# The last plain c and x step of a decoder layer written as a pair of products, with four attention tiles kept in DRAM

## The chip, the cores and the metric

The kernel is one program on one core of a Trainium2 chip. The metric is the device time of one execution in microseconds; lower is better. The engines are named as the profile names them: PE (TensorE, matmuls), PEld (its weight loads), DVE (VectorE), ACT (ScalarE), POOL (GpSimd) and SP (SyncE, which here only issues DMA).

## The reference

One layer of a hybrid decoder runs over 512 prompt tokens and 8 x 8 decode tokens, 576 columns in all, with model width 1024 and everything in fp32. Cut to what matters:

```python
h = _rmsnorm(x, norm1_g) * (1.0 + sc1) + sh1
proj = h @ w_in        # columns: b_gate, c_gate, xa (1024 each), q 1024, k 256, v 256, ga, gb (1024 each)
u = c_gate * xa
uc, new_conv = _causal_conv(u, conv_buf, conv_w)          # width 3
ya = (b_gate * uc) @ w_conv_out
o, k_state, v_state = attend(q, k, v, attn_sinks)         # window 128, 16 heads in 4 groups, sinks, ALiBi
yb = o @ w_attn_out
mixed = sigmoid(ga) * ya + sigmoid(gb) * yb
x = x + g1 * (mixed @ w_mix_out)
h2 = _rmsnorm(x, norm2_g) * (1.0 + sc2) + sh2
a, val = split(h2 @ w_up)
ac, new_ffn = _causal_conv(a, ffn_buf, ffn_conv_w)
x = x + g2 * ((gelu(ac) * val) @ w_down)
```

The outputs are the two results, the new convolution states, and the last 128 key and value rows of the prompt and of each decode sequence.

## The kernel before

**Products.** Activations lie transposed: 1024 channels are 8 tiles (`k`) of 128 partitions by 576 token columns. A column tile `m` of a weight matrix is 128 outputs wide and is loaded as one tile `raw` of 128 x 1024. An fp32 product is made of three passes with operands that are split into a high part and a low part: high weights by high activations, high by low, low by high. Splitting is a rounding on ACT (`whi <- raw`) and a subtraction on DVE (`wlo <- raw, whi`). A plain product (`product`) runs 8 k by 3 passes by the 2 column groups 0:256 and 256:576, 48 matmuls.

**Pairs.** `pair_product` computes two plain products by seven products of half the depth on half the columns, in the manner of Strassen and Winograd: seven parts of 4 k by 3 passes on 288 columns, 84 matmuls, into the three PSUM banks X, Y and Z. Between the parts, ACT writes a bank's negative into another (`minus`), and evictions (`out_a0`, `out_a1`, `out_b0`, `out_b1`) add or subtract the copy `p5`. The activations' sums (`t`, `n1`, `n3`, `n4`) are made once. Each pair needs its own weight operands: two raw tiles and their sums, in the steps `sums1 ah al bh bl dh dl sums2 ch cl` of `pair_weights`. A letter in its argument `moved` chooses another engine for a low part: for "D", ACT writes the negated high part into `wl` and POOL issues a DMA that adds the fp32 tile `s` to it. A `Job` holds one pair: `load` issues its raw loads on SP, `prepare` gives the weight steps by the number of the part behind which they stand.

**The order of the work around the change.** The first projections are six plain steps, `for at, m in enumerate(PLAIN)`. Each is a product for c, a product for x, their elementwise product `u`, and the short convolution of `u`. Beside steps 1 to 3 the queries come as three pairs (`Q_PAIRS`). Then come 18 jobs, all pairs: 14 on `w_in` and 4 on `w_conv_out`. While a job runs, the next one is prepared and the one after that is loaded. Attention is a generator that is advanced by `tick`, which every k of a product and the first k of every part calls: `filler[1]` is the rate of attention steps by tick, .4 in the last plain step and .35 from the decode tokens on. It interleaves scores (`aux <- kh, q`), a softmax on DVE and ACT, the turn of the probabilities on TensorE by the identity (`aux <- ident, s`), their copies `pt` and the products with V (`aux <- pt, V`). `prompt_values` copies attention's results to the tiles `ot` (two for each of the four key heads), which stay on the chip until the attention output product reads them after the jobs.

A scheduler orders the instructions of an engine, except where the engine is in the list `pinned`: its instructions then stay in the order of the code. POOL's and SP's loads in this stretch are in program order too. In before PE, ACT and DVE join the list ahead of the last plain step's x product. There are 57 tiles of 128 x 576 or less to share (`A_BUFS`), 4 raw tiles, 5 tiles each for high and low weights, and PSUM banks in two groups, `mm` and `aux`.

In the profile most operations carry one line, L114, since a helper records them; after the change it is L115. The results' copies `ot` are L1196 (after: L1199), the products with V L1185 (L1187), the cache copies to the output on POOL L1476 (L1490).

Of the kernel before, what the change touches and what calls it, by code (L numbers as in the profile page):

```python
# [10 lines left out]
F32 = mybir.dt.float32  # L11
# [5 lines left out]
P = 128  # L17
D = 1024
NK = D // P
# [11 lines left out]
ROWS_AHEAD = 5  # L31
PLAIN = (0, 1, 2, 4, 5, 6)
Q_TICKS = 8
Q_PAIRS = (1,2,3,)
OPS_AT = 1, 2, 3, 4
CACHE_AT = 17,18
# [38 lines left out]
def step_kernel(ctx: ExitStack, tc: tile.TileContext, ins: dict, outs: list):  # L75
    nc = tc.nc
# [18 lines left out]
    def slot(s, dt=F32, shape=None):  # L95
        return ap_.tile(shape or [P, NT], dt, tag="a", name=nm(s))
# [7 lines left out]
    pinned = []  # L104
# [78 lines left out]
    def weights(src, nk):  # L183
        return split_w(load_w(src, nk))
# [305 lines left out]
    def pair_product(w, x, steps, out_a0, out_a1, out_b0, out_b1, apart=False):  # L490

        X, Y = (halves(mmps())[1][:, :HT] if apart or n else aux()[:, :HT] for n in range(2))
        Z = aux()[:, :HT]
        p5 = slot("p5")[:, :HT]

        def part(bank, wn, xn_, more=True):

            (hi, lo), xs = w[wn], x[xn_]  # L500
            for k in range(4):
                xh, xl = xs[k]
                passes = (hi(k), xh), (hi(k), xl), (lo(k), xh)
                for n, (wt, xx) in enumerate(passes):
                    matmul(
                        bank, wt, xx, start=not more and k + n == 0, stop=k + n == 5,
                        skip_group_check=more,
                    )
                if k == 0:
                    tick(2)  # L510

        def minus(out, src):
            act.activation(out, src, AF.Copy, scale=-1.0)

        parts = [
            (X, "a0", "x00", lambda: minus(Y, X)),
            (Z, "s1", "n1", lambda: act.copy(p5, Z)),
            (Y, "s2", "t2", lambda: minus(Z, Y)),
            (X, "a1", "x10", lambda: out_a0(X)),
            (Y, "s3", "n3", lambda: out_b1(Y, p5, ALU.subtract)),  # L520
            (Z, "s4", "x11", lambda: out_a1(Z, p5, ALU.add)),
            (Y, "b1", "n4", lambda: out_b0(Y)),
        ]
        if 0 in steps:
            steps[0]()
        for at, (bank, wn, xn_, after) in enumerate(parts):
            part(bank, wn, xn_, at > 1)
            after()
            if at + 1 in steps:
                steps[at + 1]()  # L530

    def kpm(w, m0, k0=0, nk=NK):
        return w[k0 * P : (k0 + nk) * P, m0 : m0 + P].rearrange("(k p) m -> p k m", p=P)
# [476 lines left out]

    pinned.append(pe)
    ot = []
    od = []

    def softmax_steps(s, n, sinks, nsinks, w):
# [161 lines left out]
    def prompt_values(parts):  # L1177
        O = aux()
        while len(ot) < 2 * parts[-1][0] + 2:
            ot.append(slot("ot"))  # L1180
        for u, (hd, i, pts) in enumerate(parts):
            nkt, c = len(pts), slice(256 * u, 256 * u + 256)
            for n in range(2 * nkt):
                kt, par = n // 2, n % 2
                done = nc.tensor.matmul(  # L1185
                    O[HALF[par], c],
                    vt(i - nkt + 1 + kt)[:, hd * 64 : hd * 64 + 64],  # L1187
                    pts[kt][:, par * 256 : par * 256 + 256],
                    start=(kt == 0), stop=(kt == nkt - 1),
                )  # L1190
                if u + n:
                    tc.keep_in_program_order(done)
        for u, (hd, i, pts) in enumerate(parts):
            for g in range(2):
                at = 256 * u + P * g
                nc.scalar.copy(ot[2 * hd + g][:, i * P : i * P + P], O[:, at : at + P])  # L1196

    def attention():
        units = [(hd, i) for hd in range(4) for i in range(4)]  # L1199
# [154 lines left out]
    def joined(*parts):  # L1354
        out = {}
        for part in parts:
            for at, fs in part.items():
                out.setdefault(at, []).extend(fs)
        return {at: (lambda fs=fs: [f() for f in fs]) for at, fs in out.items()}
# [40 lines left out]
    def copy_outs(ts):  # L1400
        ta, tb = ts

        def total(t):
            return lambda x, y, op: dve.tensor_tensor(out=t[:, HT:], in0=x, in1=y, op=op)

        return (
            lambda ps: act.copy(ta[:, :HT], ps), total(ta), lambda ps: act.copy(tb[:, :HT], ps), total(tb),
        )
# [22 lines left out]
    def inner_outs(m):  # L1431
        c, x, u = slot("c"), slot("x1"), padded()

        def b1(z, y, op):
            dve.tensor_tensor(out=x[:, :HT], in0=z, in1=y, op=op)

        def a1(z, y, op):
            n = 512 - HT
            dve.tensor_tensor(out=c[:, HT:], in0=z, in1=y, op=op)
            dve.tensor_tensor(out=u[:, 2 + HT : 514], in0=x[:, :n], in1=c[:, HT:512], op=ALU.mult)  # L1440
            nc.gpsimd.tensor_tensor(
                out=b10(u)[:, :, 2:10], in0=b8(x[:, n:HT]), in1=b8(sv(c)), op=ALU.mult
            )

        def b0(ps):
            dve.tensor_tensor(out=u[:, 2 : 2 + HT], in0=ps, in1=c[:, :HT], op=ALU.mult)
            keep_state(u, m, NK)

        inner[m] = lambda: branch_conv(u, m)
        return lambda ps: act.copy(c[:, :HT], ps), a1, b0, b1  # L1450
# [6 lines left out]
    def inner_job(m):  # L1457
        return Job(w_in, 1024 + m * P, made, lambda: inner_outs(m), 1024)
# [10 lines left out]
    jobs += [Job(wco, m * P, made_g, lambda m=m: conv_outs(m)) for m in range(0, NK, 2)]  # L1469


    for at, m in enumerate(PLAIN):
        if at in (4, 5):
            src, dst = ((ins["cache_k_win"], nks), (ins["cache_v_win"], nvs))[at - 4]
            tc.keep_in_program_order(
                nc.gpsimd.dma_start(  # L1476
                    dst[:, 0:120, :].rearrange("b (x w) c -> b x (w c)", x=2),
                    src[0].rearrange("b w h d -> b w (h d)")[:, 8:128, :].rearrange(
                        "b (x w) c -> b x (w c)", x=2
                    ),  # L1480
                )
            )
        w = weights(kpm(w_in, 1024 + m * P), NK)
        if 1 <= at <= 3:
            key_parts(at)
            if at in Q_PAIRS:
                qt = [slot("qt") for _ in range(2)]
                filler[1] = .2
                pair_product(q_job.w, made["op"], {}, *copy_outs(qt), True)
                filler[1] = .32  # L1490
            for n in range(2):
                queries(2 * at + n, qt[n] if at in Q_PAIRS else None)
        if at == 5 and filler:
            filler[1] = .4
        ps = product(w, h)
        if at == 0:
            stT = state_in(st_conv, "stT", NK)
        if at == 1:
            a = aux()
            transpose(a[:, :74], par2, ident[:74, :74])  # L1500
            nc.scalar.copy(par2T, a[:, :74])
        c_sb = slot("c")
        nc.scalar.copy(c_sb, ps)
        w = weights(kpm(w_in, 2048 + m * P), NK)
        steps = {}
        if at + 1 in Q_PAIRS:
            q_job = Job(w_in, Q0 + (2 * at + 2) * P, None, None)
            q_job.load()
            fs = [f for x in q_job.prepare("").values() for f in x]
            for k, n in [(0, 2), (1, 1), (2, 1), (3, 1), (4, 2), (5, 1), (6, 1), (7, 1)]:  # L1510
                steps[k], fs = fs[:n], fs[n:]
        if at == len(PLAIN) - 1:
            jobs[0].load()
        if at == len(PLAIN) - 1:
            pinned += [pe, act, dve]
            fs = [f for x in jobs[0].prepare("D").values() for f in x]
            for k, n in [(0, 2), (1, 1), (2, 1), (3, 1), (4, 2), (5, 1), (6, 1), (7, 1)]:
                steps[k], fs = fs[:n], fs[n:]
            jobs[1].load()
        ps = product(w, h, steps)  # L1520
        u = padded()
        dve.tensor_tensor(out=u[:, 2:514], in0=pv(ps), in1=pv(c_sb), op=ALU.mult)
        dve.tensor_tensor(
            out=b10(u)[:, :, 2:10], in0=b8(sv(ps)), in1=b8(sv(c_sb)), op=ALU.mult
        )
        keep_state(u, m, NK)
        inner[m] = lambda u=u, m=m: branch_conv(u, m)
        if at < len(PLAIN) - 1:
            inner[m]()
    gp = []  # L1530

    def g_at(kp, name):
# [25 lines left out]
    for n in range(4):  # L1558
        if n:
            jobs[n_conv + n].before = {  # L1560
                1: [lambda n=n: late[2 * n - 2]()], 2: [lambda n=n: late[2 * n - 1]()],
            }
    jobs[-1].after = {
        2: [lambda: part_o(2)], 3: [lambda: part_o(3)],
        4: [lambda: w_next.update({1: split_w(w_raw)})], 5: [lambda: part_o(4)], 6: [lambda: part_o(6)],
        7: [lambda: part_o(8)],
    }

    def part_o(n):
        for k in range(len(o), n):  # L1570
# [716 lines left out]
```

## Time and profile before

| | |
|---|---|
| time, median of 3 runs (lowest to highest) | 960.87 us (960.2 to 962.41) |
| the profiled execution's own time | 960.62 us |
| its span | 958.8 us |
| granted TensorE clock | 0.997 |
| PE busy | 944.6 us, 7290 matmuls |
| DVE busy | 725.8 us |
| ACT busy | 549.1 us |
| POOL busy | 132.9 us |

The span is the time between the first and the last instruction of the profiled execution; the 1.8 us between it and that execution's own time lie around the span. Busy time of PE runs from the start to the modelled end of its matmuls, so overlapping matmuls count once. A row of a timeline or of a list of groups reads: line, engine, operation, output tile `<-` input tiles, shapes, count; the numbers ahead are start and duration in us, and a bracket at the end names the idle time just before and what released the engine.

### The profile page before, as it was taken

Reading aid. Unit: us, or ns where it says so; the run is one execution under the profiler, and the core shown is the slowest. Engines: PE = TensorE matmul, PEld = TensorE weight load, DVE = VectorE, ACT = ScalarE, POOL = GpSimd, SP = SyncE. Lnnn points to the kernel's source line nnn. Section 1 sums busy time; section 2 is a strip of 40 time slices with the busy share of each in tenths; the row PEclk is TensorE's granted clock in tenths of the full one; section 3 lists DMA queues with packets and bytes.
Section 4 is the critical chain, followed back from the end, with each engine's and each line's share of the span. In section 5 each row is a group of like instructions: output and inputs, shape, how many; then the busy total and the mean of one; then the engine's idle time right before and its main releaser. Section 6 shows DMA issues by size and latency. Waiting matters only on the chain.

```text
span 958.8 us, 18738 instructions
## 1 busy us (share of the span) xinstructions
PE 944.6 (99%) x7290; PEld 909.4 (95%) x7290; DVE 725.8 (76%) x1355; ACT 549.1 (57%) x1058; POOL 132.9 (14%) x317
## 2 busy tenths in 40 slices
PE   7999999999999999999999999999999999999997
PEld 5799999999999899999889999999999999999997
DVE  4788988875876867876677588995559998968864
ACT  5474768745665447865344566653226565546664
POOL 2123121101201012210001130100000011101110
PEclk9999999999999999999999999999999999999999
DMA  9984233426546768799985732232323233228542
GB/s 275 332 249 110 77 93 100 150 71 172 122 128 201 237 220 215 198 247 285 302 282 113 185 86 66 85 106 67 110 89 90 88 90 109 84 82 173 128 96 99
DMA packets 182651, 144.09 MB, mean 150 GB/s; under 512 B 7688, under 2 KB 162124, under 8 KB 182274
## 3 DMA queue, kind: packets, MB, share of 16 engines
q1 hardware_dynamic: 172546, 111.72, 38.9%
q0 software_dynamic: 9872, 30.92, 14.1%
q8 instruction: 57, 0.93, 0.4%
q14 instruction: 32, 0.26, 0.1%
q10 hardware_dynamic: 144, 0.26, 0.1%
HBM read 113.89 MB, written 12.07 MB: 131 GB/s over the span
## 4 chain that ended last, share of the span: by engine, by line
PE 90%; DMA 3%; ACT 2%; issue 2%; DVE 1%; SPq 1%; POOL 0%; POOLq 0%; ACTq 0%; DVEq 0%
PE mm L114 50%; PE aux L114 37%; PE aux L1281 2%; PE aux L1185 2%; DMA ad<-in_w_ada 1%; SPq L538 1%; DMA wlo<-raw 1%; DMA raw<-in_w_down 1%; ACT whi L114 1%; DMA x<-in_x_prompt 1%; ACT wlo L114 0%; ACT xh L114 0%; ACT sg L114 0%; ACT nh L114 0%; DVE tl L114 0%
## 5 line engine op out<-in xcount | busy, mean ns | idle before, releaser
L114 ACT ACTIVATE whi<-raw 128x1024 fp32r<-128x1024 f32 (+3 forms) x186 | 188.8, 1023 | 81.7 <-DVE raw L114 28.4
L114 DVE TENSOR_TENSOR wlo<-raw,whi 128x1024 fp32r<-128x1024 f32 (+2 forms) x163 | 192.3, 1185 | 37.0 <-ACT whi L114 36.2
L114 PE MATMUL aux<-2l,whi 128*128 128x288 f32 (+2 forms) x232 | 68.4, 295 | 0.0
L114 PE MATMUL aux<-2h,whi 128*128 128x288 f32 (+2 forms) x232 | 68.3, 295 | 0.0
L114 PE MATMUL aux<-2h,wlo 128*128 128x288 f32 (+2 forms) x232 | 68.3, 295 | 0.0
L114 DVE TENSOR_TENSOR raw<-raw 128x512 f32<-128x512 f32 x88 | 61.6, 700 | 2.8
L114 PE MATMUL mm<-hh,whi 128*128 128x256 f32 (+2 forms) x264 | 60.6, 303 | 0.5 <-ACT hh L114 0.5
L114 PE MATMUL mm<-hh,wlo 128*128 128x256 f32 (+2 forms) x264 | 58.3, 295 | 0.0
L114 PE MATMUL aux<-hh,whi 128*128 128x288 f32 (+1 forms) x196 | 57.5, 300 | 0.0
L114 PE MATMUL mm<-hl,whi 128*128 128x256 f32 (+2 forms) x264 | 57.4, 295 | 0.1
L114 PE MATMUL aux<-hl,whi 128*128 128x288 f32 (+1 forms) x196 | 56.5, 295 | 0.0
L114 PE MATMUL aux<-hh,wlo 128*128 128x288 f32 (+1 forms) x196 | 56.4, 295 | 0.0
L114 PE MATMUL mm<-fh,whi 128*128 128x256 f32 x224 | 48.0, 296 | 0.4 <-DVE rt L114 0.4
L114 PE MATMUL mm<-fh,wlo 128*128 128x256 f32 x224 | 47.9, 295 | 0.0
L114 PE MATMUL mm<-fl,whi 128*128 128x256 f32 x224 | 47.8, 295 | 0.0
L114 PEld LDWEIGHTS mm<-hh,whi 128*128 128x128 f32 x264 | 43.8, 188 | 1.5 <-ACT hh L114 1.1
L114 PEld LDWEIGHTS mm<-hl,whi 128*128 128x128 f32 x264 | 44.0, 188 | 0.7 <-DVE hl L114 0.5
L114 PEld LDWEIGHTS mm<-hh,wlo 128*128 128x128 f32 x264 | 44.6, 188 | 0.0
L114 PEld LDWEIGHTS aux<-2h,whi 128*128 128x128 f32 x232 | 43.7, 188 | 0.0
L114 PEld LDWEIGHTS aux<-2h,wlo 128*128 128x128 f32 x232 | 43.7, 188 | 0.0
L114 PEld LDWEIGHTS aux<-2l,whi 128*128 128x128 f32 x232 | 43.6, 188 | 0.0
L114 DVE SCALAR_TENSOR_TENSOR y<-pad,par2T,y 128x592 f32<-128x592 f32 x44 | 36.6, 833 | 9.0 <-ACT y L114 8.2
(409 smaller groups left out, 3104.9 us busy)
## 6 DMA issues: line engine op xcount, KB each, us to landing
raw<-in_w_in SPq DMA_DIRECT2D x52, 512.0 KB, 4.7
raw<-in_w_up SPq DMA_DIRECT2D x44, 512.0 KB, 3.9
ada<-in_w_ada SPq DMA_DIRECT2D x64, 256.0 KB, 5.4
wlo<-raw POOLq DMA_DIRECT2D x17, 512.0 KB, 4.8
ad<-in_w_ada SPq DMA_DIRECT2D x32, 256.0 KB, 6.2
raw<-in_w_down SPq DMA_DIRECT2D x16, 512.0 KB, 4.0
sg_dram<-sg POOLq DMA_DIRECT2D x16, 288.0 KB, 4.4
gt<-sg_dram SPq DMA_DIRECT2D x16, 288.0 KB, 5.7
```

The costliest lines, as they stand in the source:

```text
L114: done = getattr(self.engine, name)(*args, **kwargs)
L538: return tc.keep_in_program_order(nc.sync.dma_start(dst, src))
L1185: done = nc.tensor.matmul(O[HALF[par], c], vt(i - nkt + 1 + kt)[:, hd * 64 : hd * 64 + 64], pts[kt][:, par * 256 : par * 256 + 256], start ...
L1281: done = nc.tensor.matmul(ps[32 * j : 32 * j + 32, :], cT[:, k, :], cols[k][j], start=(k == 1), stop=(k == NK - 2),)
```

## The change

`FIRST_PAIR = 5` makes the last plain step, number 5 with m = 6, a pair: `pair_product` with the weights of c and of x for m = 6, by the same `inner_outs` that jobs 6 and 7 use. Its job becomes the head of the row of jobs (`chain`). So its raw tiles are loaded and its weights prepared beside the x product of step 4, where jobs[0] is loaded too. During the pair itself jobs[0] is prepared and jobs[1] loaded; in before jobs[0] was prepared beside the x product of step 5. The filler's rate in the pair is .25 by tick, of which a pair has 14 where two plain products have 16. PE, ACT and DVE are pinned from the end of the loop on, so the scheduler orders the pair's instructions. The u and convolution of m = 6 go the way of the jobs' (`inner[6]` in jobs[1]).

A pair takes more tiles at a time. Four of the eight `ot` tiles, those of key heads 0 and 1, are written to DRAM (`o_dram`) by POOL when they are complete, which sets their slots free, and loaded by SP into new slots beside jobs 14 and 15.

```diff
--- before.py
+++ after.py
@@ -31,6 +31,7 @@
 ROWS_AHEAD = 5
 PLAIN = (0, 1, 2, 4, 5, 6)
 Q_TICKS = 8
+FIRST_PAIR = 5
 Q_PAIRS = (1,2,3,)
 OPS_AT = 1, 2, 3, 4
 CACHE_AT = 17,18
@@ -1010,6 +1011,7 @@
 
     pinned.append(pe)
     ot = []
+    o_dram = dp.tile([4, P, 512], F32, name="o_dram")
     od = []
 
     def softmax_steps(s, n, sinks, nsinks, w):
@@ -1193,7 +1195,10 @@
         for u, (hd, i, pts) in enumerate(parts):
             for g in range(2):
                 at = 256 * u + P * g
-                nc.scalar.copy(ot[2 * hd + g][:, i * P : i * P + P], O[:, at : at + P])
+                t = ot[2 * hd + g]
+                nc.scalar.copy(t[:, i * P : i * P + P], O[:, at : at + P])
+                if i == 3 and 2 * hd + g < 4:
+                    nc.gpsimd.dma_start(o_dram[2 * hd + g], t[:, 0:512])
 
     def attention():
         units = [(hd, i) for hd in range(4) for i in range(4)]
@@ -1469,6 +1474,15 @@
     jobs += [Job(wco, m * P, made_g, lambda m=m: conv_outs(m)) for m in range(0, NK, 2)]
 
 
+    chain = [inner_job(m) for m in PLAIN[FIRST_PAIR:]] + jobs[:2]
+
+    def ahead(n):
+        if n == 1:
+            chain[0].load()
+        chain[n].load()
+        k = n - 1
+        return chain[k].prepare("D" if chain[k] is jobs[0] else "D")
+
     for at, m in enumerate(PLAIN):
         if at in (4, 5):
             src, dst = ((ins["cache_k_win"], nks), (ins["cache_v_win"], nvs))[at - 4]
@@ -1480,18 +1494,31 @@
                     ),
                 )
             )
-        w = weights(kpm(w_in, 1024 + m * P), NK)
+        if at < FIRST_PAIR:
+            w = weights(kpm(w_in, 1024 + m * P), NK)
         if 1 <= at <= 3:
             key_parts(at)
             if at in Q_PAIRS:
                 qt = [slot("qt") for _ in range(2)]
                 filler[1] = .2
-                pair_product(q_job.w, made["op"], {}, *copy_outs(qt), True)
+                steps = {}
+                if at == FIRST_PAIR:
+                    steps = joined(ahead(1))
+                pair_product(q_job.w, made["op"], steps, *copy_outs(qt), True)
                 filler[1] = .32
             for n in range(2):
                 queries(2 * at + n, qt[n] if at in Q_PAIRS else None)
-        if at == 5 and filler:
-            filler[1] = .4
+        if at >= FIRST_PAIR:
+            if filler:
+                filler[1] = .25
+            if at == 99:
+                pinned += [pe, act, dve]
+            outs = inner_outs(m)
+            job = chain[at - FIRST_PAIR]
+            pair_product(job.w, made["op"], joined(ahead(at - FIRST_PAIR + 2)), *outs, True)
+            if at < len(PLAIN) - 1:
+                inner[m]()
+            continue
         ps = product(w, h)
         if at == 0:
             stT = state_in(st_conv, "stT", NK)
@@ -1509,14 +1536,10 @@
             fs = [f for x in q_job.prepare("").values() for f in x]
             for k, n in [(0, 2), (1, 1), (2, 1), (3, 1), (4, 2), (5, 1), (6, 1), (7, 1)]:
                 steps[k], fs = fs[:n], fs[n:]
-        if at == len(PLAIN) - 1:
-            jobs[0].load()
-        if at == len(PLAIN) - 1:
-            pinned += [pe, act, dve]
-            fs = [f for x in jobs[0].prepare("D").values() for f in x]
+        if at + 1 == FIRST_PAIR and at + 1 not in Q_PAIRS:
+            fs = [f for x in ahead(1).values() for f in x]
             for k, n in [(0, 2), (1, 1), (2, 1), (3, 1), (4, 2), (5, 1), (6, 1), (7, 1)]:
                 steps[k], fs = fs[:n], fs[n:]
-            jobs[1].load()
         ps = product(w, h, steps)
         u = padded()
         dve.tensor_tensor(out=u[:, 2:514], in0=pv(ps), in1=pv(c_sb), op=ALU.mult)
@@ -1525,8 +1548,9 @@
         )
         keep_state(u, m, NK)
         inner[m] = lambda u=u, m=m: branch_conv(u, m)
-        if at < len(PLAIN) - 1:
-            inner[m]()
+        inner[m]()
+    if act not in pinned:
+        pinned += [pe, act, dve]
     gp = []
 
     def g_at(kp, name):
@@ -1560,11 +1584,19 @@
             jobs[n_conv + n].before = {
                 1: [lambda n=n: late[2 * n - 2]()], 2: [lambda n=n: late[2 * n - 1]()],
             }
+    jobs[15].after = {1: [lambda: reload_o(3)]}
+    jobs[14].after.setdefault(1, []).extend([lambda: reload_o(0)])
+    jobs[14].after.setdefault(3, []).extend([lambda: reload_o(1)])
+    jobs[14].after.setdefault(5, []).extend([lambda: reload_o(2)])
     jobs[-1].after = {
         2: [lambda: part_o(2)], 3: [lambda: part_o(3)],
         4: [lambda: w_next.update({1: split_w(w_raw)})], 5: [lambda: part_o(4)], 6: [lambda: part_o(6)],
         7: [lambda: part_o(8)],
     }
+
+    def reload_o(k):
+        ot[k] = slot("ot")
+        nc.sync.dma_start(ot[k][:, 0:512], o_dram[k])
 
     def part_o(n):
         for k in range(len(o), n):
```

What this does to the engines' orders shows at three places. On PE, in before, the end of the c product of the last plain step (output `mm_2853`) and the attention behind it, products of copied probabilities `pt` with V and turns by the identity:

```order
L114 MATMUL mm_2853<-hl_513,whi_2849 128x320
L114 MATMUL mm_2853<-hh_512,wlo_2850 128x256
L114 MATMUL mm_2853<-hh_512,wlo_2850 128x320
L1185 MATMUL aux_2904<-pt_2769,V_684 64x256 x2
L1185 MATMUL aux_2904<-pt_2865,V_684 64x256 x2
L1185 MATMUL aux_2904<-pt_2872,V_684 64x256 x2
L114 MATMUL aux_2917<-ident,s_2690 128x128
```

In the new order the same kind of attention step stands between the second part of the pair (bank Z, `aux_2892`) and the third (bank Y, `mm_2891`):

```order
L115 MATMUL aux_2892<-t_718,whi_2765 128x288
L115 MATMUL aux_2892<-t_719,whi_2765 128x288
L115 MATMUL aux_2892<-t_718,wlo_2766 128x288
L1187 MATMUL aux_2984<-pt_2792,V_684 64x256 x2
L1187 MATMUL aux_2984<-pt_2909,V_684 64x256 x2
L1187 MATMUL aux_2984<-pt_2916,V_684 64x256 x2
L115 MATMUL mm_2891<-t_718,whi_2854 128x288
L115 MATMUL mm_2891<-t_719,whi_2854 128x288
L115 MATMUL mm_2891<-t_718,wlo_2855 128x288
```

Matmuls of 256 and 320 columns on the plain operands `hh` and `hl` have become matmuls of 288 columns, here on sums `t`, with a bank change every 12; six rows of V (twelve matmuls) stand ahead of part 3.

On POOL, in before, the last plain step, from the clearing of its pad and the cache copy to the low weights `wl` that belong to jobs[0]:

```order
L1229 MEMSET pad_2835 128x2
L1237 COPY pad_2835<-stT 128x8x2
L1476 DMA out<-in_cache_v_win 8x2x15360
L1258 COPY sto<-pad_2835 128x2
L1259 COPY sto<-pad_2835 128x16
L114 DMA wl_3018<-s_2960 128x512
L1229 MEMSET pad_3073 128x2
```

After:

```order
L1490 DMA out<-in_cache_v_win 8x2x15360
L1263 COPY sto<-pad_2870 128x2
L1264 COPY sto<-pad_2870 128x16
L1234 MEMSET pad_2884 128x2
L1242 COPY pad_2884<-stT 128x8x2
L115 DMA wl_2802<-s_2746 128x512
L115 DMA wl_2959<-s_2894 128x512
L1446 TENSOR_TENSOR pad_2884<-x_2883,c_2882 128x8x8
```

`wl_2802` is the pair's own low weight and is new, `wl_2959` is that of jobs[0]; the pad of m = 6 is now cleared ahead of both and filled on POOL itself. Further up on the same queue, in before, transfers of q of the last key heads:

```order
L947 DMA q_2317<-low_2316 64x512
L947 DMA q_2318<-low_2316 64x512
L947 DMA q_2328<-low_2327 64x512
L947 DMA q_2329<-low_2327 64x512
L1229 MEMSET pad_2575 128x2
```

After:

```order
L948 DMA q_2320<-low_2319 64x512
L948 DMA q_2321<-low_2319 64x512
L1201 DMA o_dram<-ot_2075 128x512
L1201 DMA o_dram<-ot_2076 128x512
L948 DMA q_2331<-low_2330 64x512
L948 DMA q_2332<-low_2330 64x512
L1234 MEMSET pad_2580 128x2
```

The two writes of key head 1's results have moved in between the two pairs of q transfers; those of key head 0 stand likewise among the q transfers of an earlier step.

## The prediction

> **What bounds the kernel now.** I read the page first, then the windows around the place of the change, the waits of TensorE, and the timelines of the four engines there. The page, with its engine totals, its row of slices and its chain:
>
> ```profile
> span 958.8 us, 18738 instructions
> PE 944.6 (99%) x7290; PEld 909.4 (95%) x7290; DVE 725.8 (76%) x1355; ACT 549.1 (57%) x1058; POOL 132.9 (14%) x317
> PE   7999999999999999999999999999999999999997
> PE 90%; DMA 3%; ACT 2%; issue 2%; DVE 1%; SPq 1%; POOL 0%; POOLq 0%; ACTq 0%; DVEq 0%
> ```
>
> TensorE is busy in all but 14.2 us of the span, and what is missing lies in the first and the last slice. The question for any edit in between is how many matmuls it takes away and whether TensorE ever has to wait for the others in return. The windows (columns after the stretch: its length, then busy time and count of PE, PEld, DVE, ACT, POOL, the granted clock, DMA share, GB/s) are those of the step before the change, of the changed step, and of the first pair behind it:
>
> ```profile
> 180.00:200.00 20.00, 20.00 (x153) 18.70 (x152) 15.06 (x50) 12.49 (x44) 1.19 (x5) 1.00 0.24 82
> 200.00:226.50 26.50, 26.50 (x210) 23.73 (x208) 16.29 (x40) 14.17 (x40) 2.36 (x8) 1.00 0.39 117
> 226.50:250.00 23.50, 23.45 (x202) 22.13 (x201) 16.20 (x34) 15.76 (x33) 4.82 (x8) 1.00 0.54 138
> ```
>
> PE fills the first two to the last hundredth at a granted clock of 1.00; DVE is busy 61% and ACT 53% of the second. So the step is bound by TensorE, and it leaves the helpers some 10 to 12 us. The list of what TensorE waited for over the whole run says the same; these are its first row and the longest waits for an ACT eviction:
>
> ```profile
> PE aux L114 <- POOL ident masks.py:199: 4.4, 1, 4.4
> ...
> PE mm L114 <- ACT aux L114: 0.4, 2, 0.2
> ...
> PE mm L114 <- ACT mm L114: 0.3, 1, 0.3
> ```
>
> **The change part by part.** *The matmuls.* A plain step is two products, c and x, of 8 k by 3 passes by 2 column groups: 96 matmuls of 256 and 320 columns. The pair is seven parts of 4 k by 3 passes: 84 matmuls of 288 columns. The chain has clean stretches of both: 96 plain matmuls early on, 396 in the middle, and the regular pairs behind (24 + 12 + 12 + 12 + 12 + 12 from one start to the next):
>
> ```profile
> 66.85 12.65 PE mm L114 x96
> ...
> 653.36 52.65 PE mm L114 x396
> ...
> 761.57 3.19 PE aux L114 x24
> ...
> 772.67 3.19 PE aux L114 x24
> ```
>
> 96 plain matmuls cost 12.65 us, or 96 x 52.65 / 396 = 12.76 us by the longer row; 84 of the pair 772.67 - 761.57 = 11.10 us. That is a saving of 1.55 to 1.66 us; I take 1.60. The mean width is 288 columns on both sides, so it is the 12 fewer matmuls at about 0.132 us each.
>
> *What lies between them.* TensorE's timeline has the start of the old c product, the attention's values and turns that stand inside the step, and the start of the first job behind it:
>
> ```profile
> 207.65 0.43 PE L114 MATMUL mm<-hh,whi 128*128 128x256 f32 x2
> ...
> 213.37 1.52 PE L1185 MATMUL aux<-pt,V 128*64 128x256 f32 x12
> 214.82 1.09 PE L114 MATMUL aux<-ident,s 128*128 128x128 f32 x8
> ...
> 226.53 0.40 PE L114 MATMUL aux<-hh,whi 128*128 128x288 f32 x1
> ```
>
> The step lasts 226.53 - 207.65 = 18.88 us, 12.7 of them products and 6.2 attention. In the new order eight turns, twelve value matmuls and eight turns stay inside the pair (0.8 + 1.45 + 0.8, from the two rows, the tails overlapping); a further eight turns and sixteen value matmuls go behind the pair's end, into the first job. They are moved, not saved. The new step lasts 11.1 + 3.05 = 14.2 us, and the first job starts near 221.8.
>
> *The preparation.* The pair's weights need sums, differences and more roundings than the plain ones. From the stretch 180 to 250 by shape:
>
> ```profile
> L114 ACT ACTIVATE whi<-raw 128x1024 fp32r<-128x1024 f32 x8 | 8.6, 1070 | 4.4 <-PE aux L114 4.4
> L114 DVE TENSOR_TENSOR wlo<-raw,whi 128x1024 fp32r<-128x1024 f32 x7 | 8.5, 1221 | 4.5 <-ACT whi L114 4.5
> L114 DVE TENSOR_TENSOR raw<-raw 128x512 f32<-128x512 f32 x6 | 4.2, 692 | 0.2
> L114 ACT ACTIVATE wl<-wh 128x512 fp32r<-128x512 f32 x3 | 1.9, 629 | 0.1
> L114 POOL DMA_DIRECT2D wl<-s x3 | 2.8, 942 | 15.6 <-ACT wl L114 15.6
> ```
>
> Counted by the new order and priced with these rows, DVE gets about 5.5 us more (1.5 lo roundings at 1.22, four sums at 0.69, 0.9 of evictions that were ACT's), ACT 2.8 us more, POOL one weight issue and four writes of attention results. With 16.29 + 5.5 = 21.8 us in the 26.5 - 1.6 = 24.9 us that are left, DVE would be busy 88% of the stretch: it fits, if the order is right. On the path it costs nothing as long as each piece is ready when TensorE comes to it, so I walk the three tightest.
>
> These rows show what the old order had at those moments (ACT, DVE, DVE, ACT, POOL):
>
> ```profile
> 212.47 0.56 ACT L1173 COPY pt<-aux 128x512 f32<-128x512 f32 x1
> 213.00 1.15 DVE L1038 TENSOR_SCALAR s<-s,den 128x256 f32<-128x256 f32 x4
> 219.17 1.23 DVE L114 TENSOR_TENSOR wlo<-raw,whi 128x1024 fp32r<-128x1024 f32 x1 [2.56 <-ACT whi L114]
> 222.04 0.63 ACT L114 ACTIVATE wl<-wh 128x512 fp32r<-128x512 f32 x1
> 222.97 0.97 POOL L114 DMA_DIRECT2D wl<-s  x1 [13.57 <-ACT wl L114]
> ```
>
> (1) Part 3 starts near 207.65 + 1.59 + 0.8 + 1.59 + 1.45 = 213.1 and needs ACT's negated copy of part 1, which ACT reaches between its exponentials near 212.0: 1.1 us to spare; the value matmuls ahead of it need copies of turned scores that are ready about 1.0 us early. (2) The eight turns behind part 4, at 216.3, need DVE's scaling, which the row has ending at 214.15: 2.1 us. (3) Part 5, at 217.1, needs weights whose low half is rounded by ACT near 209.7, issued by POOL in 0.97 us, and summed in by DMA. The landing times:
>
> ```profile
> wl<-s POOLq DMA_DIRECT2D x16, 256.0 KB, 4.0
> ...
> out<-in_cache_v_win POOLq DMA_DIRECT2D x1, 960.0 KB, 6.9
> raw<-in_w_attn_out SPq DMA_DIRECT2D x8, 512.0 KB, 6.8
> ```
>
> 209.7 + 1.0 + 4.0 = 214.7, so 2.4 us to spare; the 960 KB copy of the cache ahead of it on that queue was issued at 203.1 and landed by 210. The first job's weights have 1.4 to 2 us. I find no wait of TensorE that the order forces, and take 0; the least slack is 1.0 us, so a slip of 2 us in ACT's or DVE's order would cost 1.0. Below nothing it cannot go, since TensorE was already full in the stretch.
>
> *The attention results by DRAM.* Two pairs of POOL writes stand among transfers of q. Rows of ACT, POOL, TensorE, POOL and the DMA list:
>
> ```profile
> 139.14 0.58 ACT L1196 COPY ot<-aux 128x128 f32<-128x128 f32 x3
> ...
> 139.79 0.52 POOL L947 DMA_DIRECT2D q<-low  x1 [0.20 <-DVE den L1035]
> ...
> 146.55 0.22 PE L114 MATMUL aux<-kh,q 128*128 128x128 f32 x1
> ...
> 177.40 0.52 POOL L947 DMA_DIRECT2D q<-low  x1 [2.40 <-DVE low L943]
> ...
> q<-low POOLq DMA_DIRECT2D x16, 128.0 KB, 2.4
> ```
>
> The first pair is ready at 139.72 and takes two issues of 0.52 to 1.0 us ahead of the q issued at 139.79: landing is 142.2 + 1 to 2 us, the use 146.55, so 0. The second pair falls into the 2.40 us that POOL waited ahead of 177.40: 0, at worst 1 us if its copies come late. The reloads stand on SP a job of 11.1 us or more ahead of their use; the slowest load of a similar kind takes 6.8 us: 0.
>
> *The sum* is made against the profiled run's own 960.62 us (span 958.8 and 1.8 around it), 0.25 us under the median of 960.87. 960.62 - 1.60 = 959.0; on the median 960.87 - 1.60 = 959.3. About 0.2%, 1.9 us, is what a measurement of this kernel can tell from no change, and 1.60 us is 0.17%: a gain that stays just inside it.
>
> **The rivals.** *A: POOL is held up by DVE, and the pair's low weights are late.* In before one of POOL's small copies shows such a hold beside a DVE sum, against the same copy earlier:
>
> ```profile
> 209.06 0.19 POOL L1258 COPY sto<-pad 128x2 f32<-128x2 f32 x1 [5.41 <-DVE pad L114]
> ...
> 226.97 0.71 POOL L1258 COPY sto<-pad 128x2 f32<-128x2 f32 x1 [0.48 <-DVE pad L114]
> ...
> 226.96 0.68 DVE L114 TENSOR_TENSOR s<-raw,raw 128x512 f32<-128x512 f32 x1
> ```
>
> The copy took 0.71 us in place of 0.19, as long as DVE's sum beside it. In the new order POOL clears and copies a pad just ahead of the weight issue, while DVE is nearly full. If each of those three is held for one lo rounding of 1.22 us, the weights land at 214.7 + 3.7 = 218.4, 1.3 us after part 5 wants them: 960.87 - 1.60 + 1.3 = 960.6, and with ACT's slip of 1.0 us on top 961.6. For it speaks the row; against it that there is a pair of such issues at every job, where TensorE shows no wait. [...]
>
> *B: DVE is the bound of the step, and it is slower.* Place: DVE from the last scores of the step before to the first job, where two pairs' preparations now stand beside five softmax units. Price: if none of the 5.5 us that DVE gains is hidden, 960.87 - 1.60 + 5.5 = 964.8. It decides from the point where more than 1.6 + 1.9 = 3.5 us of them show. For it speaks the 88%, and that DVE takes its work in order, so a sum that waits for its raw load stops the softmax behind it. Against it: the five gaps in DVE's old order, one of them the 2.56 us above, which such work can fill, and the slacks of 1 to 2.4 us.
>
> *C: the change doesn't do what it says.* If the twelve matmuls were not on the path, the time stays 960.9. TensorE at 26.50 of 26.50 us speaks against it; 2%.
>
> **How the numbers follow.** Nothing waits: 60%, 959.3, with its own range of 958.4 to 960.2, from the 0.1 us between the two rows of the plain step and a scatter of the median (the three runs lie between 960.2 and 962.41). A: 20%, 960.2 to 961.6. B: 18%, 962.8 to 964.8. C: 2%. Of the first case nearly half falls below 960.87 - 1.92 = 958.95 by scatter alone, since 959.3 is only 0.35 from that bound: 0.28 of it counts as faster, 0.32 as the same. A and C are the same but for 0.02, and B is slower but for its lower end. Faster 0.29, same 0.53, slower 0.18. The range of 8 in 10 goes from 958.3 to 962.6: it leaves out most of B and a little at the lower end.
>
> **What would show it.** Right: TensorE's span from the end of the step before (near 207.65) to the first job's first matmul is 14.2 us in place of 18.9, with 84 matmuls and no idle, and all later landmarks come 1.6 us earlier, the regular pairs still 11.10 us apart. A shows as a gap of PE ahead of part 5, released by a DMA into the low weights; B as gaps in the pair or in the first two jobs, released by DVE, with DVE without idle in front of them; a late reload as a wait in the attention's output product. The prediction is wrong if TensorE loses over 3.5 us in these places, or gains over 2.5.

## The result, and the profile after

The changed kernel takes 965.0 us (median of 10 runs, 963.72 to 968.47) against 961.32 us before (10 runs, 959.61 to 962.41): 1.0041 times as long, 95% interval 1.0032 to 1.0051. That is 3.7 us slower, where 1.6 us faster was forecast, and 2.4 us above the upper end of the forecast range. The page of its profiled execution (963.72 us):

```profile
span 961.9 us, 18719 instructions
PE 943.1 (98%) x7278; PEld 907.7 (94%) x7278; DVE 729.9 (76%) x1362; ACT 552.7 (57%) x1064; POOL 136.2 (14%) x323
PE   6999999999999998999999999999999999999997
```

TensorE has 12 matmuls fewer and is busy 1.5 us less, as the arithmetic says, and the span is 3.1 us longer. So it waited. The row of slices says where: the sixteenth of 40 slices, 361 to 385 us, has an 8 where before had 9. That is some 150 us behind the pair. The windows of the pair show that nothing happened there (columns as in the prediction):

```profile
200.00:222.80 22.80, 22.80 (x179) 20.98 (x178) 19.66 (x46) 17.89 (x46) 4.57 (x12) 1.00 0.58 160
222.80:246.30 23.50, 23.50 (x195) 22.04 (x194) 15.93 (x28) 15.33 (x27) 4.81 (x8) 1.00 0.77 190
```

PE is full to the last hundredth, and DVE is busy 19.66 of 22.80 us, 86%, without TensorE waiting for it. The list of TensorE's waits has two entries, three waits in all, that before doesn't have behind its head:

```profile
PE aux L1286 <- DMA ada<-in_w_ada: 3.7, 2, 3.2
...
PE aux L115 <- DMA wlo<-raw: 0.8, 1, 0.8
```

The tile `ada` holds weights of the adaLN modulation. 2048 of the modulation's columns, those of g1 and sh2 (line 1286, before 1281), are computed in the second part of the same filler that carries the attention: `beside_conv` yields all attention steps and then the 32 weight tiles and 64 matmuls of this modulation. In the chain of waits, the first wait and what led to it, and the second:

```profile
367.11 6.09 DMA sg_dram<-sg
...
373.28 0.69 ACT xh L115
...
374.01 5.04 DMA ada<-in_w_ada
...
379.09 1.92 PE aux L1286 x16
...
411.98 7.49 DMA wlo<-raw
```

SyncE waited 6.8 us ahead of the load of the modulation's last weight tile, for the write of a gate tile `sg` to DRAM. Nothing but the slot joins these two tiles. Two such writes were issued at 367.11 and 367.67; the first landed at 373.2 and released ACT's `xh`, which the chain has in between, the second at 373.9, and the load left at 374.01. It landed at 379.05, 3.2 us after TensorE came to it. SyncE's timeline, before and after, has the load at the end of a group of three that stretches while it waits:

```profile
298.57 0.94 SPq L1297 DMA_DIRECT2D ada<-in_w_ada  x2
...
356.52 8.50 SPq L1297 DMA_DIRECT2D ada<-in_w_ada  x3
```

```profile
308.07 1.02 SPq L1302 DMA_DIRECT2D ada<-in_w_ada  x2
...
365.28 9.05 SPq L1302 DMA_DIRECT2D ada<-in_w_ada  x3
```

The modulation's first load is issued 9.5 us later than before, almost a job, and the last three begin 8.8 us later and at another place of the jobs. In before the last load waited for a slot too, 7.2 us, but for one that a matmul gave free, by the profile; it left at 364.68, landed at 368.83, and TensorE came to it at 371.06, 2.2 us later. In the changed kernel it left 9.3 us later and took 5.0 us in place of 4.1, while TensorE came to it only 4.8 us later: that turns 2.2 us to spare into 3.2 us of wait.

Waits of 3.2, 0.8 and 0.5 us, less the pair's 1.6 and 0.4 us that the head of this execution happened to be shorter, make 2.5 of the span's 3.1 us. The other 0.6 stay open. The third wait, at 459.87, is for a tile of the next modulation, which another filler loads behind the reloads.

### The profile page after: what moved, and what is told of

It is laid out like the page before. It is cut to its first block, busy times and chain, and to the rows that moved or that the text cites. A ratio compares the mean times of both kernels' runs of the same rounds, so it can differ in the third digit from the quotient of the medians.

```text
span 961.9 us, 18719 instructions
## 1 busy us (share of the span) xinstructions
PE 943.1 (98%) x7278; PEld 907.7 (94%) x7278; DVE 729.9 (76%) x1362; ACT 552.7 (57%) x1064; POOL 136.2 (14%) x323
## 3 DMA queue, kind: packets, MB, share of 16 engines
q0 software_dynamic: 10336, 32.23, 14.5%
## 4 chain that ended last, share of the span: by engine, by line
PE 91%; DMA 5%; issue 1%; SPq 1%; ACT 1%; DVE 0%; POOL 0%; POOLq 0%; ACTq 0%
PE mm L115 51%; PE aux L115 37%; PE aux L1187 2%; PE aux L1286 1%; DMA ad<-in_w_ada 1%; DMA ada<-in_w_ada 1%; SPq L539 1%; DMA wlo<-raw 1%; DMA sg_dram<-sg 1%; DMA x<-in_x_prompt 1%; ACT whi L115 0%; DVE ol L115 0%; ACT s L1030 0%; ACT oh L115 0%; ACT wlo L115 0%
## 5 line engine op out<-in xcount | busy, mean ns | idle before, releaser
L115 DVE TENSOR_TENSOR wlo<-raw,whi 128x1024 fp32r<-128x1024 f32 (+3 forms) x164 | 193.7, 1187 | 33.9 <-ACT whi L115 33.0
L115 PE MATMUL mm<-hh,whi 128*128 128x256 f32 (+1 forms) x240 | 56.1, 304 | 0.5 <-ACT hh L115 0.5
L115 PE MATMUL mm<-hh,wlo 128*128 128x256 f32 (+1 forms) x240 | 53.8, 295 | 0.0
L115 PE MATMUL mm<-hl,whi 128*128 128x256 f32 (+1 forms) x240 | 52.9, 296 | 0.0
L115 PEld LDWEIGHTS mm<-hh,whi 128*128 128x128 f32 x240 | 40.0, 188 | 1.5 <-ACT hh L115 1.0
L115 ACT ACTIVATE aux<-mm 128x288 f32<-128x288 f32 x45 | 17.8, 395 | 40.8 <-PE mm L115 40.1
L115 PEld LDWEIGHTS mm<-hh,wlo 128*128 128x128 f32 x240 | 40.8, 188 | 0.0
```

Of the source, the lines that this page charges most:

```text
L115: done = getattr(self.engine, name)(*args, **kwargs)
```

## The experiments

**Theory 1, the shift.** The pair advances the attention by 14 x .25 = 3.5 steps where the plain step advanced it by 16 x .4 = 6.4. The filler is one chain, so decode attention and modulation stand later, and the modulation's last tile gets its slot too late. **Theory 2, the detour.** The writes and reloads of four attention tiles hold queues and slots.

*1. More attention inside the pair.*

```diff
-                filler[1] = .25
+                filler[1] = .5
```

> The changed kernel with the attention advanced faster inside the new pair (rate .5 by tick in place of .25, so 7 steps in place of 3.5; the old plain step gave 6.4). Theory 1, the shift: the 3.2 us wait for the modulation's weights near 376 us comes from attention, and with it the first modulation, standing about a job later; with the rate up it starts where it did before and the wait goes: about 965.0 - 3.2 = 961.8, or 960.5 if the two smaller waits go too, unless the pair itself starts to wait. Theory 2, the DRAM detour of four attention tiles holds the queues and slots: the wait stays, 964.5 to 965.5.

Measured: 966.32 us, 1.0057 (1.0043 to 1.007). The wait near 376 us is gone, as theory 1 says, and the total is no better. TensorE's timeline at the pair and two windows from there on:

```profile
219.83 0.40 PE L115 MATMUL mm<-n3h,wh 128*128 128x288 f32 x1 [1.68 <-ACT aux L115]
...
221.56 2.19 PE L115 MATMUL aux<-ident,s 128*128 128x128 f32 x8 [1.07 <-DVE s L1040]
```

```profile
215.00:225.00 10.00, 7.25 (x43) 6.53 (x42) 6.73 (x15) 7.83 (x19) 0.88 (x1) 0.78 0.61 177
225.00:235.00 10.00, 10.00 (x68) 8.62 (x68) 3.99 (x7) 2.94 (x8) 0.84 (x3) 0.88 0.59 170
```

With twice the attention the pair waits 2.75 us for ACT and DVE, and the granted clock, 1.00 before, is 0.78 and 0.88 in the 20 us from there: another 2.2 + 1.2 = 3.4 us. The sum 961.3 - 1.6 + 2.75 + 3.4, with 0.7 us of smaller waits, is 966.6.

*2. The kernel before with less attention in the last plain step.*

```diff
-            filler[1] = .4
+            filler[1] = .26
```

> The kernel before, nothing changed but the attention's rate in the last plain step, .26 in place of .4 (4.2 steps in place of 6.4), which puts the modulation's pieces about where the changed kernel has them. Theory 1: a wait of TensorE for the modulation's weights of 2 to 4 us appears near 375 us though there is neither a pair nor a detour: about 961.3 + 3 = 964.3. Theory 2: no change, 961 to 962.

Measured: 973.51 us, 1.0122 (1.0107 to 1.0136), 9 us more than theory 1 asked for. The waits and the windows at the first of them:

```profile
PE mm L114 <- DVE g L114: 3.9, 1, 3.9
PE aux L1281 <- DMA ada<-in_w_ada: 2.9, 1, 2.9
```

```profile
250.00:255.00 5.00, 1.61 (x13) 1.37 (x11) 3.91 (x11) 3.73 (x9) 0.51 (x1) 0.86 0.51 129
255.00:260.00 5.00, 4.45 (x18) 4.45 (x19) 3.27 (x7) 0.00 (x0) 0.52 (x1) 0.50 0.30 89
```

The modulation's wait, 2.9 us, is there without pair or detour: the shift is enough for it. A longer wait, 3.9 us for DVE in the jobs near 255 us, came on top; that the attention's late steps meet the jobs' evictions there is likely, but no run tests it. Behind both waits the clock fell, to 0.50 behind the first (255 to 260 us) and to 0.67 around the end of the second (385 to 390 us).

*3. The pair without the detour.* The lines with `o_dram` and `reload_o` are taken out of the changed kernel, nothing else.

> The changed kernel without the detour: the four attention tiles stay on the chip, nothing else changes. Theory 1: the 3.2 us wait stays; at most the 0.8 us wait for a low weight near 419 us goes: 964 to 965. Theory 2: the waits go, 960 to 961.

Measured: 975.36 us, 1.0148 (1.0132 to 1.0164).

```profile
PE aux L1284 <- DMA ada<-in_w_ada: 7.5, 1, 7.5
...
PE mm L115 <- DVE g L115: 2.6, 1, 2.6
```

Both theories missed by over 10 us. Theory 2 falls with its main claim: the detour doesn't make the wait. Without it, with four tiles fewer to share, the modulation's tile waits 7.5 us in place of 3.2, and the jobs wait for DVE (2.6 us) and ACT (1.3 us) ahead of it. Theory 1 was right that the wait stays, but had no price for the missing tiles.

*4. The detour without the pair.* The same lines put into the kernel before.

> The kernel before with the detour alone: the four tiles written by POOL and reloaded by SP at the same jobs, the last plain step as before. Theory 1: at most 1.3 us, the two smaller waits: 961.3 to 962.6. Theory 2: 963.5 or more.

Measured: 961.73 us, 1.0013 (1.0003 to 1.0022).

```profile
PE aux L114 <- DMA wlo<-raw: 1.0, 1, 1.0
```

The total is within what theory 1 expected. Of theory 2 this much stays: the wait near 418 us is there without the pair, so it is the detour's.

*5. The rate between.* `filler[1] = .35` in the pair.

> The changed kernel with the attention's rate in the new pair between the two tried, .35 (4.9 steps in place of 3.5 or 7). Theory 1, the shift: the modulation's last piece stands about where the kernel before has it, so the 3.2 us wait near 376 us is gone or under 0.5; what the pair itself waits lies between the changed kernel's 0 and the 2.8 us of rate .5. 960.5 to 963. Theory 3, that the pair has no room for more attention than it got: as much is lost in the pair, in waits and in a lower granted clock behind them, as is won: 965 or more.

Measured: 965.8 us, 1.006 (1.0046 to 1.0075). A miss for theory 1, and what theory 3 said: the pair waits 2.1 us for DVE's scaling, and a wait of 1.9 us for the modulation's tile is still there; the mean clock from 221 to 231 us is 0.83. Between the pair's waits and the modulation's neither of the rates tried wins against .25, so more attention inside the pair is no cure.

*6. The modulation faster, the pair as it is.*

```diff
-        filler[1] = 40 / 84
+        filler[1] = 48 / 84
```

> The changed kernel with the pair's rate as it is (.25), and the first modulation behind the attention advanced faster: 48/84 steps by tick in place of 40/84, so it starts as late but ends about where the kernel before ends it. Theory 1: the wait near 376 us is gone, the pair does not wait: 965.0 - 3.2 = 961.8, or less. If instead the modulation's tiles lack slots wherever it stands, the wait is as long elsewhere: 964 to 966.

Measured: 959.9 us, 0.999 (0.9981 to 0.9999): 5.1 us less than the changed kernel by this one number, or 4.7 with each taken against the runs of before beside it. The modulation's matmuls begin at 327.6 us, 7.4 us later than before, and its last piece stands at 370.1, 1.0 us earlier than before. Its last load left SyncE at 356.09, 14 us ahead of that piece, in a group that doesn't wait for a gate tile's write:

```profile
353.45 3.24 SPq L1302 DMA_DIRECT2D ada<-in_w_ada  x5
```

The windows where the changed kernel lost its time are full:

```profile
360.00:370.00 10.00, 10.00 (x77) 9.93 (x75) 7.61 (x13) 7.57 (x14) 2.89 (x4) 1.00 0.96 237
370.00:380.00 10.00, 10.00 (x79) 8.48 (x78) 6.21 (x12) 6.19 (x11) 1.77 (x2) 1.00 0.65 159
```

*7. The reloads later and apart*, in the changed kernel:

```diff
-    jobs[15].after = {1: [lambda: reload_o(3)]}
-    jobs[14].after.setdefault(1, []).extend([lambda: reload_o(0)])
-    jobs[14].after.setdefault(3, []).extend([lambda: reload_o(1)])
-    jobs[14].after.setdefault(5, []).extend([lambda: reload_o(2)])
+    jobs[15].after = {1: [lambda: reload_o(0)], 5: [lambda: reload_o(1)]}
+    jobs[16].after = {1: [lambda: reload_o(2)], 5: [lambda: reload_o(3)]}
```

> The changed kernel with the four reloads one to two jobs later and apart (two in each of jobs 15 and 16, at parts 1 and 5, in place of three in job 14 and one in 15). If the 0.8 us wait near 418 us for a low weight summed by DMA comes from the burst of reloads and gate loads just ahead of it, it goes: 964.2. If it comes from elsewhere, 965.0. More than 965.5 would mean the reloads then come too late for their use.

Measured: 964.73 us, 1.0038 (1.0025 to 1.0051). The total can't tell 0.8 us here, but the list of waits can: the entry for `wlo` is gone, the one for `ada` stays.

```profile
PE aux L1286 <- DMA ada<-in_w_ada: 3.1, 1, 3.1
```

In the changed kernel three reloads left SyncE within 1.5 us, among four gate loads, and the sum of a low weight on POOL's queue took 7.49 us to land beside them. The same transfer took 5.9 us in the kernel before and 7.7 in run 4; here the four of its kind between 400 and 440 us have a median of 5.7, where those of the changed kernel have 7.5.

*8. Both cures together.*

> Both edits together: the changed kernel with the modulation's rate at 48/84 and the reloads late and apart. If the pair's gain of 1.6 us is all there and both waits (near 376 and near 418 us) are gone: 960.9 - 1.6 = 959.3 or a little less than the 959.9 of the rate alone. If reloading late costs something elsewhere: 960.5 or more.

Measured: 958.22 us, 0.997 (0.9962 to 0.9979), the fastest of all: 3.2 us under the kernel before and 6.8 under the changed one. This is more than the 1.6 us of the matmuls. In the profiled executions, the stretch from the first query pair to the regular pairs of the feed-forward part, which holds every edit, is 1.3 us shorter than before's (617.8 against 619.1 us from TensorE's timelines), with a wait of 0.5 us for the next modulation's tile still in it; 1.1 us more lie ahead of it and 0.6 behind it, where both kernels do the same. Why the median has them too is open.

*9. The faster modulation in the kernel before.*

> The kernel before with nothing but the modulation's rate at 48/84. It has no wait there to lose, so if the rate only repairs what the change broke, the time stays at 960.9 (960.4 to 961.4). If the rate is a gain by itself, 959.5, and the repaired change would owe it that.

Measured: 961.62 us, 1.0004 (0.9995 to 1.0013). The rate by itself is worth nothing; it repairs what the change broke.

## Why the prediction was wrong

*Right: the matmuls and the walk.* The pair and the attention inside it take 14.5 us from 208.32 to 222.83, where 14.2 was forecast. No part waits. DVE is busy 86% where 88% was forecast. The regular pairs stand 11.16 us apart in this execution, where 11.10 was forecast; they stand 11.12 apart in run 8, with the same code there, so this is not the edit's. POOL issued the pair's low weights in time, near the 209.7 of the forecast:

```profile
209.97 0.97 POOL L115 DMA_DIRECT2D wl<-s  x1 [0.19 <-issue]
```

*Rivals A and B did not come.* No wait for low weights or for DVE in the pair or the first jobs. POOL's two copies and the fill of the pad ahead of the weight issue took 0.19, 0.21 and 0.21 us, so the hold of which A is made up, three times 1.22 us by my estimate, did not show there. What rival B said of DVE's limit showed in the pair only when more attention was put into it (waits for DVE of 1.1 us in run 1 and 2.1 us in run 5), and in the jobs without the detour (2.6 us in run 3).

*Wrong: "They are moved, not saved."* I priced the attention that leaves the step at zero, because TensorE has to do it anyway. That holds for TensorE's time. It says nothing of what stands behind it in the same chain: the filler lost 2.9 steps, and the modulation, whose first load leaves 85 us behind the pair, was issued 9.5 us later, among the gate jobs' writes, where its last tile got its slot too late to land before TensorE came to it. The term missing from the sum is the wait of 3.2 us at 376 us. Run 6 shows it: let the modulation end where it ended before, and the wait is gone and 4.7 to 5.1 us come back; run 9 shows that the same edit is worth nothing without the change. That more than 3.2 us come back is in part the two smaller waits, 0.4 us and none there in place of 0.8 and 0.5; the rest is open. Whether the wait of 0.5 us at 459 us comes from the shift is not shown: with both cures (run 8) it is there again. I had named neither the modulation nor its loads on SyncE, though both stand behind the moved steps in the same chain.

*Wrong, smaller: the detour at 0.* The reloads were on time, as forecast. What I had not priced is their burst on the DMA engines, beside which another transfer took 7.5 us to land and came 0.8 us late (7.7 us and 1.0 us late in run 4, no wait in run 7 with the reloads apart).

*Wrong in size: a wait costs its own length.* The rivals were priced so. The three waits make 4.5 us in the profiled execution, where the clock stayed at 1.00 behind them (380 to 390, 417 to 422 and 459 to 470 us). That was the fastest of the ten; the two at 963.7 us have mean clocks of 0.999 and 1.000, and the other eight, 964.3 to 968.5, have 0.993 to 0.999. These means also hold what the clock does at the head and the end of the program (0.85 from 10 to 20 us and 0.82 from 950 us on in the kernel before, 1.00 and 0.96 in the changed one), so they only hint at a loss behind the waits. Run 7, with nearly the same wait, shows one:

```profile
375.00:380.00 5.00, 1.86 (x18) 1.63 (x20) 1.59 (x4) 1.49 (x3) 0.00 (x0) 1.00 0.93 201
380.00:390.00 10.00, 10.00 (x66) 8.13 (x67) 6.64 (x11) 5.43 (x9) 1.55 (x3) 0.83 0.42 137
```

That is 1.7 us more for one wait; the median of the changed kernel lies 1.3 us above its profiled run. Of the kernel's 3.7 us, -1.6 us of matmuls and 4.5 us of waits make 2.9. That the other 0.8 is what the clock loses behind the waits in most executions fits run 7, but only the fastest execution was profiled, so it is not shown.

## What to carry to other kernels

When an edit changes how far a background chain advances, follow the chain to its end: far from the edit, its last transfer may get its slot after the time when its data are due, though it waited for a slot before without harm. Where one stretch gets less of the background work, give the next one a higher rate, and look at the place of the last piece, not at that of the first. On TensorE, where it is hardly ever idle, price a new wait at a range and not at its length alone: behind 2.75 us of waits run 1 lost 3.4 us more by the clock, 2.2 times the waits in all, behind 3.1 us run 7 lost 1.7 us more, and behind 3.2 us the changed kernel's profiled execution lost none.

## What the runs showed of the hardware

The granted clock of TensorE fell behind waits as short as 1.7 us with one of 1.1 close behind (run 1: 0.78 and 0.88 in the two windows of 10 us) or one of 2.1 us (run 5: 0.83 in 10 us), and to 0.50 behind one of 3.9 us (run 2). Behind the 3.1 us of run 7 it fell (0.83 in 10 us), behind the 3.2 us of the changed kernel's profiled execution it did not (1.00 from 380 to 390 us), nor behind the second wait of run 5, 1.9 us (1.00 from 370 to 400 us). In TensorE's timeline of run 1, matmuls of 128x288 start 0.24 us apart from 223.79 to 227.15 us, where they start 0.13 us apart ahead of the waits (216.40 to 217.85 us). What decides whether the clock falls behind a wait, with 3.1 us on one side and 3.2 us on the other, no run here shows.
